# A hybrid attention and convolution layer: the first stage's loads and engine orders laid anew, squares shared between two engines

## The chip, the core and the metric

The kernel runs on one core of a Trainium2 chip. The metric is the device time of one execution in microseconds, here 587.03 as the median of three runs (586.88 to 587.10). A core has five engines with a queue each, and each engine takes its own instructions in order: TensorE (PE; PEld is its weight load), VectorE (DVE), ScalarE (ACT), GpSimd (POOL), and SyncE (SP), which here only issues transfers.

## The reference

One layer over 1024 latent tokens and 256 context tokens, 1024 wide, in fp32. Both inputs are normalised over the row, modulated with a scale and a shift that come from a conditioning vector, and projected; columns go to eight heads of neighbourhood attention and to a gated short convolution.

```python
shift, scale, gate = adaln(c, w_ada, b_ada)
shift_c, scale_c, gate_c = adaln(c_ctx, w_ada, b_ada)
h = rmsnorm(x, norm_g) * (1 + scale[:, None]) + shift[:, None]
hc = rmsnorm(ctx, norm_g) * (1 + scale_c) + shift_c
q, k, v, za, u, bg, cg, zc = jnp.split(h @ w_in, SPLIT_POINTS, axis=-1)
...
attn = neighbourhood_attention(q, k, heads(v), kc, vc, rpb) * jax.nn.silu(za)
conv = gated_short_conv(u, bg, cg, zc, conv_w, conv_b)
x_new = x + gate[:, None] * (jnp.concatenate([attn, conv], axis=-1) @ w_out)
```

Here `rmsnorm` multiplies by the inverse root of the mean of the squares of a row, and `adaln` is a product of a silu with a weight matrix.

## The kernel before

The program has stages: a first one that makes the modulated input `h` and, from it, the first group of convolution columns; projections of the four head pairs (`pacc`, `cacc` for the context); the attention, with the other convolution columns (`pu`) as filler between its steps; the output product (`pout`). The change touches the first stage alone.

**What the first stage computes.** `h` is needed turned, with the 1024 model columns on the partitions, as eight tiles `h0` to `h7` of 128 columns, each with two halves of 512 tokens, and each as a rounded high part and a low remainder, so that three fast products replace one in fp32. The row sums of squares come from the eight token tiles x0 to x7 (`sq`, into `sums0` for the first half and `sums1` for the second; `sums2` is the context's, from n0 and n1). `root` adds a small constant on VectorE and raises to the power -0.5 on POOL; `Rt` spreads the four sums of a half over the partitions by four transposes on TensorE (two for the context), and `R` copies the result out of PSUM on ACT (`rs0`, `rs1`, `rs2`). For each column tile k, `pr` multiplies the conditioning vector with a slab of `w_mod` (64 small matmuls into `tr`), `tp` turns the result on VectorE, and `ab` makes the scale and the shift. Then for half h and tile k: `u` scales the transposed input (the loaded tile `t`, or, for two tiles of the first half, TensorE's own transposes `T` and `v`), `hi` adds the shift and rounds on ACT, `lo` takes the remainder on VectorE.

**The first columns.** Chunk k of the weights (load `c`, rounding `ch` on ACT, remainder `cl` on VectorE) meets `h` in `fc`: `fc` h k i is three matmuls of 512 columns into the banks `acc`, where i is 0 for high by high, 1 for the low weights, and 2 for the low `h`. There are 48 such groups, 144 matmuls. `conv0` evacuates the banks for the convolution: a copy `ub` on ACT and a product `cu` on VectorE for the first half of the tokens, and the same again for the second. Meanwhile the weight chunks of the first `pacc` tile are loaded and split (`q`, `qh`, `ql`), and the rotary tables are loaded (`g`) and multiplied with the gains (`rg`, VectorE).

**What sets the order.** Nothing is scheduled: `LOADS` and `STEPS` (lines 36 to 49) list short words, `do` (line 750) runs them one by one through the table `does` (line 732), and the class `ordered` chains each engine's instructions in that order. A word's loads go into SP's queue where the word stands. Buffers come in rings: three for slabs, six for `xh`, five for weight chunks `wr`, so that a load can also wait for the release of an earlier tile. Words `warm` and `fill` are matmuls on zeros with no use but to keep TensorE busy.

Of the kernel before, what the change touches and what calls it, by code (L numbers as in the profile page):

```python
# [10 lines left out]
F32 = mybir.dt.float32  # L11
F32R = mybir.dt.float32r
BF16 = mybir.dt.bfloat16
AF = mybir.ActivationFunctionType
ALU = mybir.AluOpType
# [4 lines left out]
P = 128  # L20
D = 1024
T = 1024
L = 256
KT = D // P
# [8 lines left out]
TICKS = [2, 3, 3, 4, 4, 4, 4, 1] + [4, 4, 4, 1] + [4, 4, 4, 2] + [4, 4, 4, 1] + 3 * [4, 4, 3, 1] + [3, 2, 3, 1]  # L33
EPS = 1e-6

LOADS = "x0 x1 x2 x3 s0 c0 s1 c1 x4 x5 x6 x7 t10 t11 s2 t02 t12 c2"
STEPS = [
# [11 lines left out]
]  # L49
CONTEXT = "Hi0 Hi1 Lo0 Lo1 Hi2 Hi3 Lo2 Lo3 Hi4 Hi5 Lo4 Lo5 Hi6 Hi7 Lo6 Lo7"  # L50

# [4 lines left out]
def body(tc, es, x, xb, xt, cb_, ct, w_mod, w_gate, b_ada, w_grp, w_col, q_g, k_g, bias, w_out, vecs, cst, out):  # L56
# [21 lines left out]
    pe, act, dve, pool = every = [ordered(e) for e in (nc.tensor, nc.scalar, nc.vector, nc.gpsimd)]  # L78
    sp = ordered(nc.sync)

    def sbuf(name, side=None, bufs=1):
        kw = {} if side is None else {"side": side}
        return tc.tile_pool(name=name, bufs=bufs, reuse_waits="tile", **kw)
# [59 lines left out]
    c2 = cp.tile([P, KT, 2], F32, name="c2")  # L143
    ab = cp.tile([P, KT, 4], F32, name="ab")
    ng, bsh, bsc = vecT[:, 16:24], vecT[:, 24:32], vecT[:, 32:40]
# [12 lines left out]
    def more_h(ks):  # L158
        for k in ks:
            t = place(k, [P, 2, T], F32R, f"h{k}")  # L160
            hh.append(t[:, 0])
            hl.append(t[:, 1])

    cvp = hs.enter_context(sbuf("cvp", side="right"))
# [380 lines left out]
    xp = xs.enter_context(sbuf("xp"))  # L545
# [4 lines left out]
    def tr():  # L550
        return ps0.tile([P, 512], F32, name="tr", tag="tr", bufs=2)

    strict[:] = every + [sp]
    xn, xh, xc, slabs, mods, rows, chunks, pair = {}, {}, {}, {}, {}, {}, {}, []
# [26 lines left out]
    sums = [xp.tile([P, 4], F32, name=f"sums{i}") for i in range(3)]  # L581
    spread_r = [xp.tile([P, 512], F32, name=f"rs{i}") for i in range(2)] + [cxp.tile([P, L], F32, name="rs2")]

    def square(t):

        sqj = xp.tile([P, D], BF16, name="sqj", tag="sqj", bufs=1)
        act.activation(sqj, xn[t], AF.Square, scale=1.0 / 32, accum_out=sums[t // 4][:, t % 4:t % 4 + 1])

    def root(g):

# [4 lines left out]
    def spread_rows(g):  # L595

        n = 4 if g < 2 else 2
        pr = tr()
        for i in range(n):
            pe.transpose(pr[:, i * P:(i + 1) * P], sums[g][:, i:i + 1].broadcast_to([P, P]), ident)  # L600
        return lambda: act.copy(spread_r[g][:, :n * P], pr[:, :n * P])

    def products(k):

        mods[k] = tr()
        for kt in range(KT):
            for g in range(4):
                pe.matmul(mods[k][32 * g:32 * g + 32, :64], c32[:, kt], slabs[k][:, kt, 64 * g:64 * g + 64],
                          start=kt == 0, stop=kt == KT - 1, skip_group_check=True)

    def turned_rows(k):
        rows[k] = xp.tile([P, 64], F32, name="rw", tag="rw", bufs=2)
        dve.transpose(rows[k], mods[k][:, :64])

    def modulation(k):

        a = ab[:, k].rearrange("p (w j) -> p j w", w=2)
        dve.tensor_scalar(a[:, 1], rows[k][:, 32:34], b1[:, k:k + 1], ng[:, k:k + 1], ALU.add, ALU.mult)
        dve.tensor_scalar(a[:, 0], rows[k][:, 0:2], bsh[:, k:k + 1], None, ALU.add)

    scaled = {}

# [39 lines left out]
    def half_of(v, half):  # L662
        return v[:, half * 512:(half + 1) * 512]

    def first_columns(half, k, i):

        wh, wl = chunks[k][:2]
        for u in (0, 2, 1):
            uc = slice(u * P, (u + 1) * P)
            pe.matmul(acc0[u][half], (wl if i == 1 else wh)[:, uc], half_of(hl[k] if i == 2 else hh[k], half),  # L670
                      start=k == 0 and i == 0, stop=k == KT - 1 and i == 2)

    def cast_chunk(raws, k):
        raw = raws[k][:].rearrange("p a b -> p (a b)")
        w = wpp.tile([P, 2, 384], F32R, name="w", tag="w", bufs=12)
        act.copy(w[:, 0], raw)
        raws[k] = raw, w

    def rest_of_chunk(raws, k):
        raw, w = raws[k]  # L680
        dve.tensor_tensor(w[:, 1], raw, w[:, 0].bitcast(F32), ALU.subtract)
        raws[k] = w[:, 0], w[:, 1], w[:, :, P:384]

    ch = {}

# [11 lines left out]
    tables = []  # L697

    def gains(i):

        rw, gqk = tables[0]
        if i == 0:
            pool.tensor_scalar(gqk[:, 0], gqk[:, 0], 0.125, None, ALU.mult)
            pool.tensor_tensor(gkc1[:, 0], gqk[:, 0], gqk[:, 1], ALU.mult)
            tables.append(sl.tile([P, 2, NB, 2, HD], F32, name="rg", tag="slab", bufs=3))
        n, k = divmod(i, 2)
        rraw = rw[:, 512 * n:512 * n + 512].rearrange("p (b d) -> p b d", d=HD)
        dve.tensor_tensor(tables[1][:, n, :, k], rraw, gqk[:, k:k + 1].broadcast_to([P, NB, HD]), ALU.mult)
        if i == 3:
            sp.dma_start(rope_d, tables[1][:].rearrange("p n b k d -> p (n b k d)"))  # L710

    def context_high(k):
# [11 lines left out]
    def keep_clock(n, late=False):  # L724

        v = zeros[:].rearrange("p (o n) -> p o n", o=1).broadcast_to([P, 4, P]) if late else warm
        ps = acc0[1][1][:].rearrange("p (a n) -> p a n", a=4) if late else acc0[1][1]
        for _ in range(n):
            pe.matmul(ps, zeros if late else warm[:, :P], v, start=True, stop=True)
# [4 lines left out]
        "c": lambda k: chunks.update({k: chunk_load(CU, k)}), "q": lambda k: ch.update({k: chunk_load(CQ, k)}),  # L734
        "e": lambda k: load_ct(k), "g": lambda i: tables.append(gains_load()),
        "sq": lambda t: square(t), "root": lambda g: root(g),
        "Rt": lambda g: copies.update({g: spread_rows(g)}), "R": lambda g: copies[g](),
        "pr": lambda k: products(k), "tp": lambda k: turned_rows(k), "ab": lambda k: modulation(k),
        "ch": lambda k: cast_chunk(chunks, k), "cl": lambda k: rest_of_chunk(chunks, k),
        "qh": lambda k: cast_chunk(ch, k), "ql": lambda k: rest_of_chunk(ch, k),  # L740
        "u": lambda h, k: scale((h, k), xh[h, k][:], spread_r[h][:], k, 0) if (h, k) in xh else scale_early(k),
        "T": lambda t: transposed(t), "fill": lambda n: keep_clock(n, True), "v": lambda h, k: normed_early(k), "more": lambda: more_h(range(6, KT)),
        "hi": lambda h, k: shift_high((h, k), half_of(hh[k], h), k, 0),
        "lo": lambda h, k: shift_low((h, k), half_of(hl[k], h), half_of(hh[k], h), k, 0),
        "fc": lambda h, k, i: first_columns(h, k, i), "rg": lambda i: gains(i),
        "warm": keep_clock, "Hi": lambda k: context_high(k), "Lo": lambda k: context_low(k),
        "conv": lambda i: conv_step(),
    }

    def do(steps):  # L750
        for word in steps.split():
            name = word.rstrip("0123456789")
            at = word[len(name):]
            does[name](*([int(at)] if name in ("warm", "fill") else map(int, at)))
# [9 lines left out]
    more_h(range(6))  # L764
    do(LOADS)
    keep_clock(6)
# [357 lines left out]
    tiles, scales, waiting, nxt, raws = {}, {}, [], [], []  # L1124
# [26 lines left out]
    for n in range(NT + 3):  # L1151


        p, t = divmod(n, NB)
# [23 lines left out]
        if t == 0 and 0 < n < NT:  # L1178
            nxt += map(chunk_split, raws)
            ch, nxt, raws = nxt, [], []  # L1180
# [133 lines left out]
    with sbuf("att") as ap, psum("psb") as psb:  # L1314
# [6 lines left out]
        for n in range(len(TICKS)):  # L1321
# [11 lines left out]
            if ready:  # L1333
                p = ready.pop()
# [83 lines left out]
    def four(tags):  # L1418
        return [bank("pout", tag) for tag in tags]
# [65 lines left out]
    a = four("SSCC")  # L1485
    c5 = four("OOUU")
# [29 lines left out]
    c3 = four("OOUU")  # L1516
# [84 lines left out]
```

## Time and profile before

| what | value |
|---|---|
| median of three runs | 587.03 us |
| the profiled execution | 587.34 us |
| its span, first to last instruction | 585.6 us |
| TensorE busy, 0 to 27.23 us | 22.52 us |
| TensorE busy, 27.23 to 63.16 us | 35.69 of 35.93 us |
| TensorE busy, 63.16 us to the end | 519.02 of 522.44 us |
| VectorE and ACT busy, 27.23 to 63.16 us | 28.70 and 18.30 us |
| moved by transfers, 0 to 27.23 us | 364 GB/s |

Durations are those of one execution, read from the hardware profiler. Matmuls are pipelined and their ends are modelled, so that a busy TensorE is not one at its peak, and lengths of single matmuls overlap; start-to-start steps are the better measure. A row of a timeline has the start, the length, engine, line, operation, what it writes and reads, and in brackets the idle time before it with what ended that. In the chain of waits each row is a piece of the chain that ended last: start, length, what. All the helpers' instructions carry one line, so that tiles, not lines, tell them apart.

### The profile page before, as it was taken

To read this page: it belongs to the slowest core of one execution; us is meant where nothing else is said; L and a number is where in the kernel's file an instruction comes from. 1 tells how busy PE (TensorE), PEld (TensorE's weight loads), DVE (VectorE), ACT (ScalarE), POOL (GpSimd) and SP (SyncE) were. 2 spreads that over 40 slices of the span, in tenths; PEclk is the share of its full clock that TensorE was granted. 3 is DMA by queue.
4 is the path that set the end of the run, shared out by engine and by line. 5 is a ranking of instruction groups with operands and counts; after the bars stand their busy time and mean duration, and the time that the engine had idled before them with its cause. 6 is when DMAs were issued, how large, how long until landed. Compare 5 with 4: busy or idle time off the path is not lost.

```text
span 585.6 us, 9903 instructions
## 1 busy us (share of the span) xinstructions
PE 577.2 (99%) x3531; PEld 483.3 (83%) x3532; DVE 438.6 (75%) x890; ACT 282.0 (48%) x653; POOL 57.4 (10%) x82
## 2 busy tenths in 40 slices
PE   8899999999999999999999999999999999999997
PEld 4578999999999999988878787878787867888886
DVE  1578879656846746367998788998979887999952
ACT  5636355336525545433463474466535646643420
POOL 1001033123223232100000000000000001100000
PEclk9999999999999999999999999999999999999999
DMA  8997666845756695686253646564758273773532
GB/s 323 410 415 278 220 229 211 283 166 194 267 189 213 224 341 205 226 297 219 73 209 120 243 140 229 182 216 155 254 187 257 80 263 96 248 252 89 199 125 91
DMA packets 66679, 126.14 MB, mean 215 GB/s; under 512 B 8714, under 2 KB 27650, under 8 KB 64325
## 3 DMA queue, kind: packets, MB, share of 16 engines
q1 hardware_dynamic: 66244, 124.70, 60.8%
q0 software_dynamic: 384, 0.81, 0.6%
q8 instruction: 28, 0.46, 0.3%
q14 instruction: 23, 0.18, 0.1%
HBM read 92.38 MB, written 33.10 MB: 214 GB/s over the span
## 4 chain that ended last, share of the span: by engine, by line
PE 91%; DMA 5%; DVE 2%; ACT 1%; SPq 0%; issue 0%; POOL 0%; DVEq 0%; ACTq 0%
PE pu L71 29%; PE pacc L71 23%; PE pout L71 13%; PE acc L71 5%; PE po L71 5%; PE cacc L71 4%; PE pss L71 3%; DMA xn<-in_xb 3%; PE pc L71 3%; PE pmx L71 2%; PE trA L71 1%; PE tr L71 1%; DMA y_d<-tb 1%; PE ptot L71 1%; PE trB L71 1%; DVE sb L71 0%
## 5 line engine op out<-in xcount | busy, mean ns | idle before, releaser
L71 PE MATMUL pu<-h,uh 128*128 128x512 f32 x544 | 174.4, 402 | 0.0
L71 PE MATMUL pacc<-w,h 128*128 128x384 f32 x768 | 138.5, 337 | 0.0
L71 PEld LDWEIGHTS pacc<-w,h 128*128 128x128 f32 x768 | 132.8, 188 | 0.2
L71 PEld LDWEIGHTS pu<-h,uh 128*128 128x128 f32 x544 | 97.3, 188 | 18.4 <-issue 1.2
L71 PE MATMUL pu<-h,ul 128*128 128x512 f32 x272 | 106.5, 391 | 0.0
L71 PE MATMUL pout<-right,left 128*128 128x512 f32 (+2 forms) x348 | 77.0, 383 | 0.0
L71 PEld LDWEIGHTS pout<-right,left 128*128 128x128 f32 x348 | 64.4, 188 | 12.7
L71 PEld LDWEIGHTS pu<-h,ul 128*128 128x128 f32 x272 | 51.1, 188 | 11.5
L71 POOL TENSOR_TENSOR ss<-ss,few 128x4 f32<-128x4 f32 (+1 forms) x40 | 41.4, 1035 | 127.0 <-DVE ss L71 126.7
L71 ACT COPY sc<-pc 128x512 f32<-128x512 f32 x32 | 18.7, 587 | 44.6 <-PE pc L71 44.6
L71 PE MATMUL acc<-h,w 128*128 128x512 f32 x144 | 35.3, 397 | 1.4 <-ACT h L71 1.4
L71 ACT ACTIVATE sc<-sc 128x512 f32<-128x512 f32 x32 | 20.3, 633 | 33.7 <-DVE sc L71 33.6
L71 ACT ACTIVATE sq<-pacc 128x256 f32<-128x256 f32 x32 | 12.3, 386 | 47.4 <-PE pacc L71 46.7
L71 DVE TENSOR_TENSOR sum<-sum,sb 128x372 f32<-128x372 f32 (+2 forms) x64 | 31.1, 485 | 2.7
L71 PEld LDWEIGHTS acc<-h,w 128*128 128x128 f32 x144 | 26.3, 188 | 7.8 <-ACT h L71 2.1
L71 DVE SCALAR_TENSOR_TENSOR m<-pout,ab,m 128x512 f32<-128x512 f32 (+2 forms) x34 | 22.9, 717 | 13.0 <-PE pout L71 12.9
L71 ACT ACTIVATE qn<-pacc,ss 128x64 f32<-128x64 f32 x128 | 30.0, 330 | 4.8 <-PE trA L71 2.5
L71 DVE TENSOR_TENSOR mx<-mx,sb 128x372 f32<-128x372 f32 (+2 forms) x64 | 30.8, 481 | 1.4
L71 DVE TENSOR_REDUCE ss<-sq 128x4 f32<-128x260 f32 (+1 forms) x40 | 15.7, 393 | 21.5 <-ACT sq L71 21.5
L71 DVE TENSOR_TENSOR ul<-uraw,uh 128x512 fp32r<-128x512 f32 x34 | 23.1, 685 | 10.0 <-ACT uh L71 10.0
L71 DVE TENSOR_TENSOR sb<-pss,bt 128x192 f32<-128x192 f32 (+3 forms) x48 | 27.5, 600 | 2.3 <-PE pss L71 2.2
L71 DVE TENSOR_TENSOR qs<-trA,qs 128x512 fp32r<-128x512 f32 x16 | 11.1, 691 | 21.2 <-ACT qs L71 20.2
(142 smaller groups left out, 862.8 us busy)
## 6 DMA issues: line engine op xcount, KB each, us to landing
uraw<-in_w_col SPq DMA_DIRECT2D x34, 256.0 KB, 3.8
slab<-in_w_mod SPq DMA_DIRECT2D x8, 1024.0 KB, 9.0
q_d<-qs SPq DMA_DIRECT2D x32, 256.0 KB, 4.0
k_s<-k_d SPq DMA_DIRECT2D x8, 1024.0 KB, 6.9
q_s<-q_d SPq DMA_DIRECT2D x16, 512.0 KB, 3.9
wr<-in_w_grp SPq DMA_DIRECT2D x40, 192.0 KB, 5.0
bt<-in_rpb SPq DMA_DIRECT2D x8, 564.0 KB, 6.8
xn<-in_xb SPq DMA_DIRECT2D x8, 512.0 KB
```

The lines of the kernel that those rows point to most:

```text
L71: i = emit(*a, **kw)
```

## The change

The first stage's two lists are written anew. Every word of the old lists stands in the new ones, but for the words `warm` and the number of `fill`; new is a word `sh`, the addition of the shift, which was part of `ab`. Three places show the kind of the change in the code:

```diff
-LOADS = "x0 x1 x2 x3 s0 c0 s1 c1 x4 x5 x6 x7 t10 t11 s2 t02 t12 c2"
+LOADS = "x0 x1 x2 x3 s0 c0 s1 x5 c1 x6 x4 x7 t10 c2 s2 t02"
 STEPS = [
...
-    "conv0 R2 rg1 rg2 rg3 ql7",
...
+    "qh4 ql6 fc171 ql4 conv0 qh3 fc170 ql3 qh7 qh5 ql7 fc172 ql5 conv0 root2 Rt2 rg3 R2",
 ]
...
-        sqj = xp.tile([P, D], BF16, name="sqj", tag="sqj", bufs=1)
-        act.activation(sqj, xn[t], AF.Square, scale=1.0 / 32, accum_out=sums[t // 4][:, t % 4:t % 4 + 1])
+        total = sums[t // 4][:, t % 4:t % 4 + 1]
+        if t in (1, 3, 5, 7):
+            sqv = cvp.tile([P, T + 2], F32, name="sqv", tag="cu", bufs=1)
+            dve.scalar_tensor_tensor(sqv[:, :D], xn[t], 1.0 / D, xn[t], ALU.mult, ALU.mult, accum_out=total)
+        else:
+            sqj = xp.tile([P, D], BF16, name="sqj", tag="sqj", bufs=1)
+            act.activation(sqj, xn[t], AF.Square, scale=1.0 / 32, accum_out=total)
...
         dve.tensor_scalar(a[:, 1], rows[k][:, 32:34], b1[:, k:k + 1], ng[:, k:k + 1], ALU.add, ALU.mult)
-        dve.tensor_scalar(a[:, 0], rows[k][:, 0:2], bsh[:, k:k + 1], None, ALU.add)
+
+    def shift(k):
+        a = ab[:, k].rearrange("p (w j) -> p j w", w=2)
+        act.activation(a[:, 0], rows[k][:, 0:2], AF.Identity, bias=bsh[:, k:k + 1])
...
+    done = [0, 0]
+
     def first_columns(half, k, i):
...
-                      start=k == 0 and i == 0, stop=k == KT - 1 and i == 2)
+                      start=done[half] == 0, stop=done[half] == 3 * KT - 1)
+        done[half] += 1
```

The last piece lets the groups `fc` of a half stand in any order: the first one that comes starts the sum in its banks. The gains' function likewise does its preparations at the first `rg` that comes and its store behind the fourth.

What the lists make of the engines' orders is shown at three places. In the rows, `acc00` and `acc01` are the banks of the first and the second half of the tokens for one column group (`acc10`, `acc11`, `acc20`, `acc21` for the others), and numbers behind an underscore count buffers.

TensorE, around the transposes of the second half's sums (`sums1`), before and then with the change:

```order
L71 MATMUL tr_425<-ci_106,sums1_162 128x128 x4
L71 MATMUL tr_435<-slab_202,c32_223 32x64 x32
L71 MATMUL acc01_157<-h0_170,w_321 128x512
L71 MATMUL acc21_158<-h0_170,w_321 128x512
L71 MATMUL acc11_160<-h0_170,w_321 128x512
```
```order
L70 MATMUL tr_420<-ci_106,sums1_162 128x128 x4
L70 MATMUL acc00_155<-h1_171,w_382 128x512
L70 MATMUL acc20_156<-h1_171,w_382 128x512
L70 MATMUL acc10_159<-h1_171,w_382 128x512
L70 MATMUL tr_435<-slab_202,c32_219 32x64 x32
L70 LDWEIGHTS zeros_116
L70 MATMUL acc11_160<-zeros_116 128x512
L70 MATMUL acc01_157<-h0_170,w_250 128x512
```

A group of three matmuls of the first half, the last of tile `h1`, has moved from ahead of these transposes to behind them; the product with the third slab stays ahead of the second half's first matmul.

TensorE, from the transposes of the context's sums (`sums2`) on, before (they stand among the groups of `h6`, with one more group of `h6` and the six of `h7` behind them), and then with the change, where the end of the last group of `h7` and the first `pacc` tile are shown:

```order
L71 MATMUL acc11_160<-h6_262,w_776 128x512
L71 MATMUL tr_898<-ci_106,sums2_163 128x128 x2
L71 MATMUL acc01_157<-h6_262,w_776 128x512
L71 MATMUL acc21_158<-h6_262,w_776 128x512
L71 MATMUL acc11_160<-h6_262,w_776 128x512
L71 MATMUL acc00_155<-h7_263,w_854 128x512
```
```order
L70 MATMUL acc01_157<-h7_255,w_704 128x512
L70 MATMUL acc21_158<-h7_255,w_704 128x512
L70 MATMUL acc11_160<-h7_255,w_704 128x512
L70 MATMUL tr_956<-ci_106,sums2_163 128x128 x2
L70 MATMUL pacc_1003<-w_691,h0_170 128x384 x3
L70 MATMUL pacc_1003<-w_829,h1_171 128x384 x3
```

The two transposes have moved from the middle of the last groups to the seam between the first stage and the second.

VectorE, where the context's sum stands (`TENSOR_SCALAR sums2`), before and then with the change:

```order
L71 SCALAR_TENSOR_TENSOR hw_799<-xh_569,ab_119,rs0_164 128x512
L71 TENSOR_SCALAR sums2_163<-sums2_163 128x2
L71 SCALAR_TENSOR_TENSOR hw_806<-xh_576,ab_119,rs1_165 128x512
L71 SCALAR_TENSOR_TENSOR h6_262<-hw_799,ab_119,h6_262 128x512
L71 SCALAR_TENSOR_TENSOR h6_262<-hw_806,ab_119,h6_262 128x512
```
```order
L70 TENSOR_TENSOR rg_900<-rw8_791 128x8x64 x2
L70 TENSOR_TENSOR w_896<-wr_787,w_896 128x384
L70 TENSOR_TENSOR w_923<-wr_837,w_923 128x384
L70 TENSOR_TENSOR cu_930<-acc20_156,ub_933 128x2x16x16
L70 TENSOR_TENSOR w_936<-wr_819,w_936 128x384
L70 TENSOR_TENSOR w_942<-wr_834,w_942 128x384
L70 TENSOR_TENSOR w_944<-wr_789,w_944 128x384
L70 TENSOR_TENSOR cu_930<-acc21_158,ub_951 128x2x16x16
L70 TENSOR_SCALAR sums2_163<-sums2_163 128x2
L70 TENSOR_TENSOR rg_900<-rw8_791 128x8x64
```

The sum has moved from between the two scalings of `h6` to behind the second product `cu`, which reads the finished bank of the second half.

On SP, the loads of the last weight chunks and of the tables stand behind the load of q1, whose buffer the remainder of chunk 5 (`cl5`) frees; `cl5` now stands behind `tp6` on VectorE, and the order of the words there is `tp6 sh6 cl5 q1 t07 n1 n0 t17 q6 q5 g0`.

More of the change, by code (lines that the diff above doesn't have):

```diff
@@ L663, in half_of @@
         return v[:, half * 512:(half + 1) * 512]
+    done = [0, 0]
     def first_columns(half, k, i):
-        wh, wl = chunks[k][:2]
+        raw, w = chunks[k]
+        wh, wl = w[:, 0], w[:, 1]
         for u in (0, 2, 1):
@@ L681, in rest_of_chunk @@
         dve.tensor_tensor(w[:, 1], raw, w[:, 0].bitcast(F32), ALU.subtract)
-        raws[k] = w[:, 0], w[:, 1], w[:, :, P:384]
+        if raws is ch:
+            ch[k] = w[:, 0], w[:, 1], w[:, :, P:384]
     ch = {}
@@ L701, in gains @@
         rw, gqk = tables[0]
-        if i == 0:
+        if len(tables) == 1:
             pool.tensor_scalar(gqk[:, 0], gqk[:, 0], 0.125, None, ALU.mult)
@@ L708, in gains @@
         dve.tensor_tensor(tables[1][:, n, :, k], rraw, gqk[:, k:k + 1].broadcast_to([P, NB, HD]), ALU.mult)
-        if i == 3:
+        tables.append(i)
+        if len(tables) == 6:
             sp.dma_start(rope_d, tables[1][:].rearrange("p n b k d -> p (n b k d)"))
@@ L737, in body @@
         "Rt": lambda g: copies.update({g: spread_rows(g)}), "R": lambda g: copies[g](),
-        "pr": lambda k: products(k), "tp": lambda k: turned_rows(k), "ab": lambda k: modulation(k),
+        "pr": lambda k: products(k), "tp": lambda k: turned_rows(k), "ab": lambda k: modulation(k), "sh": lambda k: shift(k),
         "ch": lambda k: cast_chunk(chunks, k), "cl": lambda k: rest_of_chunk(chunks, k),
```

19 rows, old and new, of the table STEPS are left out of this document.

## The prediction

> **What bounds the kernel now.** I read the page first, then TensorE's waits, the chain of waits over the first 66 us, and last VectorE's timeline around the end of that stretch. The page says that TensorE is busy throughout:
>
> ```profile
> span 585.6 us, 9903 instructions
> ...
> PE 577.2 (99%) x3531; PEld 483.3 (83%) x3532; DVE 438.6 (75%) x890; ACT 282.0 (48%) x653; POOL 57.4 (10%) x82
> ```
>
> Asked for everything that TensorE waited for from 63 us to the end, the trace has one row:
>
> ```profile
> PE pmx L71 <- DVE rm L71: 0.4, 1, 0.4
> ```
>
> So behind 63 us there is 0.4 us of waiting in 522. The changed code ends near 63 us, and whatever it moves the start of the second stage (the tile `pacc`) by should arrive at the end undiminished, in either direction. The question is when `pacc` starts. The chain of waits has today's answer (start, length, what):
>
> ```profile
> 9.45 12.32 DMA xn<-in_xb
> ...
> 21.85 1.16 ACT sqj L71 x2
> ...
> 23.04 0.18 DVE sums L71
> ...
> 23.29 1.03 POOL sums L71
> ...
> 24.36 0.66 PE tr L71 x4
> ...
> 25.05 0.59 ACT rs L71
> ...
> 25.66 0.76 DVE hw L71
> ...
> 26.45 0.73 ACT h L71
> ...
> 27.23 3.01 PE acc L71 x12
> ...
> 31.25 0.24 issue
> ...
> 52.83 1.03 PE tr L71 x64
> 53.86 4.30 PE acc L71 x18
> 58.16 0.22 PE tr L71 x2
> 58.38 4.78 PE acc L71 x21
> 63.16 2.97 PE pacc L71 x17
> ```
>
> Up to 27.23 the last token tile of the first half of the loads sets the pace: it lands at 9.45 + 12.32 = 21.77, then its square (ACT), the sum (DVE), the power (POOL), four transposes (PE), a copy, a scaling and a rounding follow one another. From 27.23 to 63.16 TensorE runs without a gap but the 0.24. The transfer is late because the queue is full: 399 to 416 GB/s (last column) from 5 us on.
>
> ```profile
> 0.00:5.00 5.00, 3.48 (x10) 1.20 (x11) 0.38 (x2) 2.92 (x4) 1.24 (x10) 1.00 0.50 162
> 5.00:10.00 5.00, 5.00 (x29) 2.69 (x28) 0.01 (x1) 4.11 (x9) 0.00 (x0) 1.00 1.03 399
> 10.00:15.00 5.00, 4.37 (x84) 2.37 (x84) 1.75 (x4) 1.66 (x4) 1.03 (x1) 1.00 1.02 416
> 15.00:20.00 5.00, 4.07 (x76) 3.10 (x77) 4.26 (x12) 3.79 (x6) 0.00 (x0) 1.00 1.02 411
> ```
>
> **The front.** The new order of loads puts x4 to x7 and c1 in another order among themselves, but the same transfers stand ahead of x7, which stays the fourteenth. It lands at 21.77 again. Its square is now VectorE's. No row shows a two-source VectorE operation of 1024 elements. The nearest are these:
>
> ```profile
> 70.47 0.87 DVE L71 SCALAR_TENSOR_TENSOR hw<-xc,ab,rs 128x256 f32<-128x256 f32 x2
> ```
> ```profile
> 57.41 1.41 DVE L71 SCALAR_TENSOR_TENSOR h<-hw,ab,h 128x512 fp32r<-128x512 f32 x2
> 58.74 1.02 DVE L71 TENSOR_TENSOR w<-wr,w 128x384 fp32r<-128x384 f32 x2
> 61.32 0.69 DVE L71 TENSOR_TENSOR cu<-acc,ub 128x512 f32<-128x512 f32 x1 [1.56 <-ACT ub L71]
> 61.93 1.49 DVE L71 TENSOR_TENSOR w<-wr,w 128x384 fp32r<-128x384 f32 x3
> 63.43 0.69 DVE L71 TENSOR_TENSOR cu<-acc,ub 128x512 f32<-128x512 f32 x1
> 64.04 1.88 DVE L71 TENSOR_TENSOR rg<-rw 128x512 f32<-128x512 f32 x3
> 65.84 0.55 DVE L71 TENSOR_TENSOR w<-wr,w 128x384 fp32r<-128x384 f32 x1
> ```
>
> A 256-element one is about 0.44, a 512-element one 0.70, so 1024 elements are bounded by 2 x 0.65 = 1.3 and 4 x 0.44 = 1.76; I take 1.4, against 1.16 on ACT: **+0.25**. What then runs up to the first matmul of the second half is the same chain, and as much useful work stands ahead of that matmul as before (18 `acc` matmuls, three products with a slab); one group of three only moves from ahead of the four transposes to behind them. So that matmul starts at 27.5. The work behind it is the same too: 63.16 - 27.23 = 35.93, less the 0.24 gap (I find no wait at this place, the loads being as early as before) and less the 0.22 for the two transposes, which now stand behind: the last `acc` matmul ends at 27.5 + 35.47 = **62.95**, 0.2 before today's.
>
> The shift additions that go to ACT cost nothing, ACT being busy 48%; they save VectorE 0.13 each (the step from 49.08 to 49.21 here), all of it beside TensorE's work:
>
> ```profile
> 48.60 0.25 DVE L71 STREAM_TRANSPOSE rw<-tr 128x64 f32<-128x64 f32 x1 [0.61 <-PE tr L71]
> 48.88 0.29 DVE L71 TENSOR_SCALAR ab<-rw,b,vecT 128x2 f32<-128x2 f32 x1
> 49.08 0.22 DVE L71 TENSOR_SCALAR ab<-rw,vecT 128x2 f32<-128x2 f32 x1
> 49.21 0.75 DVE L71 SCALAR_TENSOR_TENSOR hw<-xh,ab,rs 128x512 f32<-128x512 f32 x1
> ```
>
> **The end of the stage is what costs.** The two transposes of the context sums (`Rt2`) stood seven matmul groups ahead of `pacc`, fed by a sum that VectorE made at about 50 us. Now they stand between the last `acc` matmul and `pacc`, and the sum stands in VectorE's queue behind the second `cu` product. TensorE runs in order, so `pacc` waits for the sum, for POOL's power and for the transposes. When does VectorE get there? Its tail starts with the transpose of the last slab's rows (`tp7`), which needs the last product with a slab. Behind that product stand ten groups of three matmuls, 30 x 4.30/18 = 7.17, so it ends at 62.95 - 7.17 = 55.8. From there, by start-to-start steps of the rows above: transpose 0.28, gain 0.20, two scalings 2 x 0.67, `lo07` (its rounding on ACT, 0.73, lies beside the second scaling) 0.67 plus about 0.2 of waiting, which is 58.5. Then a `rg` 0.60, `lo17` 0.67, two `rg` 1.20, two `w` 1.00, `cu` 0.61, three `w` 1.50, `cu` 0.61: 6.19, so the sum starts at 64.7. From a sum to POOL is 23.29 - 23.04 = 0.25, from POOL to the transposes 24.36 - 23.29 = 1.07, and the transposes take 0.22: `pacc` at **66.25**, 3.1 after today's 63.16.
>
> One more thing can hold this tail. The first `rg` now waits for the table load, which stands on SP behind q1, whose buffer is freed only by VectorE's split of chunk 5, now behind `tp6`. By the same count back from the last slab product (its own 1.03, nine groups 6.45) `tp6` is at 48.3 and the split ends at 49.1. Behind it go seven loads, 2.16 MB or 5.3 us at 410 GB/s, two small ones, and the table, 1.3 us: not before 55.7. Issue to use took this long today:
>
> ```profile
> 45.89 0.42 SPq L71 DMA_DIRECT2D rw<-in_cst  x1
> ```
> ```profile
> 52.46 0.48 POOL L71 TENSOR_SCALAR rw<-rw 128x64 f32<-128x64 f32 x1 [1.22 <-DMA rw<-in_cst]
> ```
>
> That is 6.6 us; issued at about 52.8 the table lands at 59.4 at the latest. With POOL's 0.48 and 0.25 more, `rg` can start between 56.5 and 60.1, and VectorE gets there at 58.5: between nothing and 1.6 lost. The late end is the row nearest to it, but its queue was fuller; I take **+0.3**.
>
> Sum: 3.1 + 0.3 = +3.4. The profiled execution lasted 587.34 (span 585.6), 0.31 over the median of 587.03; added to each, 590.7 and 590.4. I predict the median, **590.4**.
>
> **The rivals.**
> The shortest wait: VectorE is ahead of my count and only what cannot be avoided is left. The `ub` copy follows the last write of its bank, two matmuls (0.48) before the end, 0.62 later `cu` (60.70 to 61.32 today), 0.61 the sum, 0.25, 1.07, 0.22: 62.95 + 2.29 = 65.24, +2.1, **589.1**. Against it: VectorE's queue as counted.
>
> ```profile
> 60.70 0.59 ACT L71 COPY ub<-acc 128x512 f32<-128x512 f32 x1 [0.23 <-PE acc L71]
> ```
>
> The table is late by the full 1.6: **591.7**.
>
> The array slows after the gap. Its first matmuls took 2.74/6 = 0.457 each, those after 4.48 only 3.20/14 = 0.229:
>
> ```profile
> 1.52 2.74 PE L71 MATMUL acc<-warm 128*128 128x512 bf16 x6 [1.52 <-POOL warm L71]
> ...
> 4.48 3.20 PE L71 MATMUL acc<-warm 128*128 128x512 bf16 x14
> ```
>
> An idle stretch from 62.95 to 66 could bring that state back; the loss would be what the start lost, 2.74 - 6 x 0.229 = 1.4: **591.8**. No gap over 0.7 us follows the start today, so the trace doesn't show how long one must be; all columns of granted clock read 1.00. [...]
>
> The other side: the second square sum was held by ACT and not by the landing that the trace puts at 21.77. ACT's square before it began here,
>
> ```profile
> 20.59 1.06 ACT L71 ACTIVATE sqj<-xn 128x1024 bf16<-128x1024 f32 x1
> ```
>
> and with 1.16 for one with its read of the sum it ended at 21.75. With two engines the front would gain up to the landing itself. The fourteen transfers are 6.78 MB; the four windows above moved 6.94 by 20.0, so x7 cannot be in before 19.6: at most 2.2 earlier, all stages shifted alike, **588.2**, and 586.9 with the shortest wait. It decides once the first matmul of the second half starts before 25.0. Against it: the chain names the transfer there, although by 0.02 us only.
>
> That the wait is not built is excluded: the rows of the order put the transposes directly ahead of `pacc`.
>
> **How the numbers follow.** The forecast 0.58, the shortest wait 0.12, late table 0.08, slow array 0.11, the front 0.11. The range reaches from below the shortest wait, 588.7, to above the slow array, 592.3; outside lie the front and a little of two costs together. A measurement of this kernel can tell about 0.2% from no change, 1.2 us, so "same" ends at 588.2. Of the front's 0.11, 0.08 are within it and 0.03 below, where both gains come together; 0.01 is added for what I don't see. Faster 0.04, same 0.08, slower 0.88.
>
> **What would show it.** In the new profile: first matmul of the second half at about 27.5; last `acc` matmul near 63 with no gap after 27.5; the two transposes at about 66 with the idle time ahead of them put down to POOL `sums`, some 3 us; the sum on VectorE directly behind the second `cu`, and no idle time on VectorE from `tp7` to it but for the table; behind 67 us no new TensorE wait. I am wrong if `pacc` starts before 65, or if TensorE waits at other places between 27 and 63.

## The result and the profile after

| what | before | with the change |
|---|---|---|
| median (runs) | 587.07 us (4: 586.88 to 588.14) | 594.20 us (4: 593.09 to 594.53) |
| ratio | 1 | 1.0114 [1.0096, 1.0132] |
| profiled execution, span | 587.34, 585.6 us | 593.09, 591.2 us |
| mean granted clock of the runs | 0.999 in the profiled one | 0.997, 0.994, 0.991, 0.991 |
| `pacc` starts at | 63.16 us | 67.25 us |
| its first 72 matmuls take | 12.50 us | 14.00 us |

The kernel is slower by 1.1%, as forecast in sign, but by twice the amount: 7.1 us where 3.4 were predicted, and outside the range that was given. The page of the changed kernel already differs in one slice of its clock row:

```profile
span 591.2 us, 9893 instructions
...
PE 578.8 (98%) x3528; PEld 484.1 (82%) x3528; DVE 443.3 (75%) x890; ACT 279.4 (47%) x653; POOL 56.2 (9%) x82
...
PEclk9999899999999999999999999999999999999999
```

A slice is 14.8 us; the fifth, from 59 to 74 us, has an 8. TensorE's busy time went up by 1.6 us with no more useful work to do: the same work took longer, which the lower clock explains, and idle time has to be looked for apart from it. It is in TensorE's waits from 27 us to the end (total, times, longest):

```profile
PE tr L70 <- POOL sums L70: 3.9, 1, 3.9
PE pmx L70 <- DVE rm L70: 0.4, 1, 0.4
PE acc L70 <- ACT h L70: 0.2, 1, 0.2
```

There is one new wait, of 3.9 us, at the transposes that now stand at the seam. Nothing else is new behind 27 us; the 0.4 at `pmx` was there before. The end of the chain of waits (start, length, what) gives the two parts of the loss:

```profile
64.83 0.60 DVE cu L70
65.44 0.09 DVE sums L70
...
65.66 1.04 POOL sums L70
...
66.74 0.51 PE tr L70 x2
67.25 14.00 PE pacc L70 x72
81.25 5.55 PE cacc L70 x32
```

Before, the same two last rows read:

```profile
63.16 12.50 PE pacc L71 x72
75.66 5.55 PE cacc L71 x32
```

`pacc` starts 67.25 - 63.16 = 4.09 later, and its first 72 matmuls take 1.50 more; `cacc` then starts 81.25 - 75.66 = 5.59 later, and the span is 5.6 longer. So the whole loss of the profiled execution is made between 63 and 81 us, and arrives at the end undiminished. The windows of 1 us say what the 1.50 are (the columns: stretch, its length, busy time of PE, PEld, DVE, ACT, POOL, granted clock, DMA share, GB/s):

```profile
65.00:66.00 1.00, 0.00 (x0) 0.00 (x0) 1.00 (x3) 0.00 (x0) 0.34 (x1) 1.00 0.00 0
66.00:67.00 1.00, 0.26 (x3) 0.26 (x3) 0.10 (x1) 0.00 (x0) 0.69 (x1) 0.98 0.13 57
67.00:68.00 1.00, 1.00 (x5) 1.00 (x4) 0.00 (x0) 0.71 (x2) 0.10 (x1) 0.50 1.06 451
68.00:69.00 1.00, 1.00 (x5) 1.00 (x5) 0.52 (x1) 1.00 (x2) 0.00 (x0) 0.50 0.97 401
69.00:70.00 1.00, 1.00 (x5) 1.00 (x4) 0.96 (x3) 0.12 (x1) 0.00 (x0) 0.50 0.36 139
70.00:71.00 1.00, 1.00 (x6) 1.00 (x5) 0.90 (x3) 0.00 (x0) 0.00 (x0) 0.81 0.06 16
71.00:72.00 1.00, 1.00 (x7) 1.00 (x7) 1.00 (x2) 0.00 (x0) 0.34 (x1) 1.00 0.40 49
```

Right behind the gap the clock is 0.50. From the means of the mixed slices it fell at 66.96 (0.98 is 0.04 us at half) and rose at 70.38 (0.81 is 0.38 us at half): 3.4 us, and nearly half of the work of that time is lost. TensorE is busy throughout these windows, with five matmuls touching each of them where seven or eight do at the whole clock; no list of waits shows that.

### The profile page after: what moved, and what is told of

It reads as the page before. It is cut to its first block, busy times and chain, and to the rows that moved or that the text cites. A ratio compares the mean times of both kernels' runs of the same rounds, so it can differ in the third digit from the quotient of the medians.

```text
span 591.2 us, 9893 instructions
## 1 busy us (share of the span) xinstructions
PE 578.8 (98%) x3528; PEld 484.1 (82%) x3528; DVE 443.3 (75%) x890; ACT 279.4 (47%) x653; POOL 56.2 (9%) x82
## 4 chain that ended last, share of the span: by engine, by line
PE 87%; DMA 6%; DVE 3%; ACT 1%; SPq 1%; issue 1%; POOL 0%; DVEq 0%; ACTq 0%; POOLq 0%
PE pu L70 29%; PE pacc L70 23%; PE pout L70 13%; PE po L70 5%; PE cacc L70 4%; PE pss L70 3%; DMA xn<-in_xb 3%; PE pc L70 3%; PE pmx L70 2%; PE acc L70 2%; PE trA L70 1%; DMA xh<-in_xt 1%; DMA wr<-in_w_grp 1%; DMA y_d<-tb 1%; PE tr L70 1%; PE ptot L70 1%
## 5 line engine op out<-in xcount | busy, mean ns | idle before, releaser
L70 PE MATMUL pacc<-w,h 128*128 128x384 f32 x768 | 140.1, 340 | 0.0
L70 PEld LDWEIGHTS pacc<-w,h 128*128 128x128 f32 x768 | 134.3, 190 | 0.1
L70 DVE TENSOR_TENSOR sb<-pss,bt 128x192 f32<-128x192 f32 (+3 forms) x48 | 27.5, 602 | 2.3 <-PE pss L70 2.2
```

The lines of the kernel that those rows point to most:

```text
L70: i = emit(*a, **kw)
```

## The experiments

Three readings of the 4.09 + 1.50 are weighed: **S**, all of it comes from the place of the context's sum and its two transposes at the seam (a wait, then the halved clock); **F**, part of it comes from the front (the squares on VectorE, the order of the first loads); **L**, part of it comes from the late table and the rest of the lists.

**The sum moved ahead, the transposes before the last group.** On the changed kernel, two words:

```diff
-    "... sq8 rg1 fc071 fc072 rg0 fc070",
-    "qh4 ... ql3 qh7 qh5 ql7 fc172 ql5 conv0 root2 Rt2 rg3 R2",
+    "... sq8 rg1 root2 fc071 fc072 rg0 fc070",
+    "qh4 ... ql3 qh7 Rt2 qh5 ql7 fc172 ql5 conv0 rg3 R2",
```

> The changed kernel, with the context's sum moved up in VectorE's queue (ahead of the last groups of the first stage) and its two transposes moved ahead of the last group, so that nothing at the seam waits for them. Theory S (the whole loss is the wait at the seam, about 4 us, and the halved clock after it, 1.5 us for each window): 587.0 within 0.6, clock 0.999, no TensorE wait between 62 and 68 us. Theory L (the late loads of the last weight chunks and tables hold the tail): pacc still waits for VectorE's splits, 588 to 590. Theory F (the front: squares on two engines, idle stretches there and clock drops they cause): 590 or more, clock below 0.998.

Measured: 588.54 us (10 runs, 587.11 to 588.99), 1.0019 [1.0009, 1.0028]. The ten runs have mean clocks of 0.997 to 1.000. Most of the loss is gone, but about 1.1 us of it stay. In this kernel's trace, VectorE's, POOL's and TensorE's timelines have (start, length, engine, what, and in brackets the idle time before it):

```profile
60.92 0.68 DVE L70 TENSOR_TENSOR rg<-rw 128x512 f32<-128x512 f32 x1
61.52 1.01 DVE L70 TENSOR_TENSOR w<-wr,w 128x384 fp32r<-128x384 f32 x2
```
```profile
61.08 2.03 POOL L70 TENSOR_TENSOR sums<-sums,few 128x2 f32<-128x2 f32 x1 [3.02 <-DVE sums L70]
```
```profile
63.17 0.43 PE L70 MATMUL tr<-ci,sums 128*128 128x128 f32 x2 [1.06 <-POOL cu L70]
```

POOL's power lasts 2.03 us, where the same instruction took 1.03 to 1.04 at the seam of the changed kernel, and the transposes wait 1.06 for it. It runs beside the rest of an `rg`, two `w` and a `cu` of VectorE; at the seam only the rest of an `rg` ran beside it. The expectation had reckoned with 1.0, and that is its miss: the power ends 1 us later than was reckoned, and the transposes stood too early by that much.

**The same early sum, the transposes left at the seam.** Against the changed kernel only `root2` has moved:

```diff
-    "... sq8 rg1 fc071 fc072 rg0 fc070",
-    "... ql5 conv0 root2 Rt2 rg3 R2",
+    "... sq8 rg1 root2 fc071 fc072 rg0 fc070",
+    "... ql5 conv0 Rt2 rg3 R2",
```

> The changed kernel, with the context's sum early in VectorE's queue and its transposes at the seam as in the changed kernel, so that POOL, which took 2.0 us for the power beside VectorE's work, is done when they come up. S: pacc directly behind the last acc group at about 63.3 us, 587.3 within 0.6: the rest of the change is worth nothing either way. If the rest of the change costs or saves something: 588.5 or more, 586.4 or less.

Measured: 587.31 us (11 runs, 586.76 to 588.19), 0.9999 [0.9990, 1.0007]. The chain of waits of this kernel:

```profile
60.95 0.17 DVE sums L70
...
61.19 2.04 POOL sums L70
...
63.29 0.42 PE tr L70 x2
63.71 12.50 PE pacc L70 x72
```

The power takes 2.04 again, but now it ends at about the end of the last group. With everything else of the change in place, one word's place in VectorE's queue makes up the 7 us, and the rest of the change, the new front included, is worth nothing that can be measured in either direction. That is against F and L.

**The squares alone**, on the kernel before: the two branches of the diff's `square`, nothing else.

```diff
+        if t in (1, 3, 5, 7):
+            dve.scalar_tensor_tensor(sqv[:, :D], xn[t], 1.0 / D, xn[t], ALU.mult, ALU.mult, accum_out=total)
+        else:
             act.activation(sqj, xn[t], AF.Square, scale=1.0 / 32, accum_out=total)
```

> The kernel before, with the squares of every second token tile on VectorE and nothing else. If the landing of x7 sets the front, as the chain says: 587.3, within 0.3 of before (VectorE's square with its read of the sum took 1.24 us against ACT's 1.16). If ACT's run of squares held it: 585 to 586.5.

Measured: 587.59 us (11 runs, 587.02 to 588.27), 1.0003 [0.9995, 1.0012]; `pacc` starts at 63.45, 0.29 later than before in the profiled execution. The squares are not where the time went, and nothing was gained by them either; that too is against F. What holds the front is not shown by this experiment: here VectorE comes to the last square at 21.97 straight from other work, and the chain of waits runs through TensorE's own queue (19 `acc` matmuls, ten of them on zeros, from 20.53 to 25.15). In the changed kernel it can be seen: VectorE stands idle for 1.36 us until the last token tile has landed at 21.76, and in eight profiles with the changed lists, where it landed between 21.28 and 22.18, the first matmul of the second half came 5.85 to 5.86 later each time.

**The kernel before, with the seam of the change.** The other direction: the two words and nothing else of the change.

```diff
-    "sq9 tp6 ... fc150 root2 u16 ..."
-    "... u17 hi07 Rt2 ql1 q6 fc162 hi17 lo07",
-    "conv0 R2 rg1 rg2 rg3 ql7",
+    "sq9 tp6 ... fc150 u16 ..."
+    "... u17 hi07 ql1 q6 fc162 hi17 lo07",
+    "conv0 root2 Rt2 R2 rg1 rg2 rg3 ql7",
```

> The kernel before, with that one move alone: the context's sum behind the second cu product, its transposes behind the last acc group. S: pacc starts 2.3 to 2.6 us later, 589.5 if the clock holds, 591 to 592.5 if the gap of 2.4 us halves it for one window or two. F or L: 587.2, no difference worth the name.

Measured: 590.28 us (4 runs: 589.92, 589.11, 590.64, 591.07, with mean clocks of 0.999, 1.000, 0.996, 0.997), 1.0049 [1.0034, 1.0064]. Its chain:

```profile
62.97 0.59 ACT ub L71
...
63.59 0.69 DVE cu L71
64.28 0.08 DVE sums L71
...
64.50 1.04 POOL sums L71
...
65.59 0.43 PE tr L71 x2
66.02 12.52 PE pacc L71 x72
```

Here VectorE has little else queued, and the wait is the least that this place allows: copy, `cu`, sum, power, transposes follow one another, and `pacc` is 2.86 late, a little more than the 2.3 to 2.6 expected. In the profiled execution the clock stayed whole (72 matmuls in 12.52); the two runs with a mean clock of 0.996 and 0.997 are the slowest. The two words alone thus make the kernel slower by about 3 us. One row of VectorE in this profile bears on the first experiment:

```profile
64.26 1.89 DVE L71 TENSOR_TENSOR rg<-rw 128x512 f32<-128x512 f32 x3
```

POOL's power ran from 64.50 to 65.54 beside these three products and took 1.04 all the same. So the power was not longer beside every product of VectorE. Beside `w` alone it was: in the front of the changed kernel, on 128x4, it took 1.25 us beside two `w` and 1.03 where VectorE was idle. Beside `cu` alone no run shows it.

**The seam filled.** The changed kernel, with sixteen matmuls on zeros, into a bank that is free, ahead of the two transposes. The wait for the sum stays, TensorE is not idle in it.

```diff
-    "... ql5 conv0 root2 Rt2 rg3 R2",
+    "... ql5 conv0 root2 seam16 Rt2 rg3 R2",
...
+    def keep_seam(n):
+        v = zeros[:].rearrange("p (o n) -> p o n", o=1).broadcast_to([P, 4, P])
+        ps = tr()[:].rearrange("p (a n) -> p a n", a=4)
+        for _ in range(n):
+            pe.matmul(ps, zeros, v, start=True, stop=True)
...
```

> The changed kernel, with 16 matmuls on zeros between the last acc group and the two transposes, into a free bank; the wait itself stays. S: pacc starts at about 67 us as in the changed kernel, but the granted clock stays 1.00 behind it and its first 72 matmuls take 12.5 us instead of 14.0; 591.3 within 0.6 and clock 0.999 in all runs. If the clock loss doesn't come from the gap (F): 594 and clock 0.991 to 0.997.

Measured: 590.87 us (4 runs: 590.36, 591.32, 591.78, 590.41), 1.0066 [1.0049, 1.0083]; mean clocks 1.000, 1.000, 0.997, 0.999. The chain of the first of them:

```profile
64.69 0.09 DVE sums L70
...
64.92 1.04 POOL sums L70
...
66.00 0.43 PE tr L70 x2
66.43 12.50 PE pacc L70 x72
```

The 72 matmuls take 12.50 again: in this execution the slow stretch is gone when TensorE is kept busy in the gap, though nothing useful is done in it. Of the four runs one still has a mean clock of 0.997, which was not expected. What stays, `pacc` at 66.43, is the wait by itself.

**The gap halved.** The changed kernel with `root2` directly behind the first `conv0`, so that the sum waits for one `cu` and not for two:

```diff
-    "... ql4 conv0 qh3 fc170 ql3 qh7 qh5 ql7 fc172 ql5 conv0 root2 Rt2 rg3 R2",
+    "... ql4 conv0 root2 qh3 fc170 ql3 qh7 qh5 ql7 fc172 ql5 conv0 Rt2 rg3 R2",
```

> The changed kernel, with the context's sum directly behind the first cu product, so that the gap at the seam is about 2 us instead of 3.9. S: pacc at about 65.2 us; 590.6 if a gap of 2 us still halves the clock for one window, 589.1 if it doesn't. F or L: 592 or more.

Measured: 590.93 us (4 runs: 589.89, 590.52, 591.96, 591.34; mean clocks 1.000, 0.999, 0.993, 0.996), 1.0062 [1.0046, 1.0078]. From the chain of the first of these executions:

```profile
63.39 1.84 POOL sums L70
...
65.27 0.43 PE tr L70 x2
65.70 12.51 PE pacc L70 x72
```

The gap is 2.5 us and the power takes 1.84 beside VectorE's products. With the whole clock the time is that of a wait of 2.5; the two runs with the lower clocks are 0.8 to 2.1 us above the two others. So a gap of 2.5 us seems to be followed by a low clock in some executions and not in others; this rests on the mean clock and the time alone, as no execution with the low clock was caught in a profile here.

**The changed kernel again**, in six, one and one more runs, to see how its executions differ.

> The changed kernel once more, for its spread over executions. If the seam is all there is, every execution has the gap of about 4 us, and the times differ by whole half-rate windows of 3.4 us (1.5 us of pacc each): 592.5 to 594.6, clock 0.991 to 0.997. If the clock is also lost elsewhere, the granted clock over the first 30 us is below 1.00 in the profile.

Measured: 592.49 us (6 runs), 1.0083 [1.0067, 1.0099]. Five of them have clocks of 0.993 to 0.997 and took 592.35 to 593.71; the sixth has a clock of 1.000 and took 590.29, like the kernel with the filled seam. The profiled one shows the picture of the first: `pacc` at 66.97, its first 72 matmuls in 13.99.

> The changed kernel unchanged, one look, in search of an execution with a mean clock under 0.996. One window at half rate of 3.41 us lowers the mean clock of a 591 us span by 0.0029, so 0.994 is two windows and 0.991 three. If the further windows belong to the seam, the profile shows the first 72 pacc matmuls longer than 14.0 (up to 15.5). If they belong to the front, where the tensor engine waits 1.7 us in pieces for the first two sums and 1.2 us for the token tiles, a granted clock of 0.5 shows between 9 and 30 us and the first matmul of the second half starts later than 27.7. Time 592.3 to 594.5; with 0.997 or more nothing is told apart.

> As the third look at the changed kernel: the same kernel, the same two readings, the same numbers.

Measured: 593.70 us at a mean clock of 0.997, and 594.12 at 0.994. The first has `pacc` at 67.74 and its first 72 matmuls in 14.07, one slow stretch. The chain of the second, and its windows of 1 us:

```profile
66.02 1.04 POOL sums L70
...
67.10 0.69 PE tr L70 x2
67.79 14.83 PE pacc L70 x72
```
```profile
63.00:64.00 1.00, 0.18 (x1) 0.00 (x0) 1.00 (x3) 0.89 (x2) 0.00 (x0) 1.00 0.03 12
...
65.00:66.00 1.00, 0.00 (x0) 0.00 (x0) 1.00 (x4) 0.00 (x0) 0.00 (x0) 0.95 0.00 0
66.00:67.00 1.00, 0.00 (x0) 0.00 (x0) 0.46 (x1) 0.00 (x0) 0.98 (x1) 0.50 0.00 0
...
72.00:73.00 1.00, 1.00 (x5) 1.00 (x5) 1.00 (x3) 0.00 (x0) 0.81 (x1) 0.64 0.82 156
```

The clock fell at 65.90, inside the gap (63.18 to 67.10), and rose at 72.72: 6.82 us, two times 3.41. The second stretch at a clock of 0.50 lies directly behind the first, at the seam, and not at the front. The first of the two still held 1.2 us of the gap; the 72 matmuls lose 2.33 us. In the three other profiles of the changed kernel, with one slow stretch, the fall came 0.22 to 0.55 us after the gap's end. So which of the two kinds an execution is goes with where the fall comes.

**The front filled, the seam open.** Thirteen more matmuls on zeros at the places where TensorE waits in the front:

```diff
-    "T1 sq2 sq1 T2 sq0 T0 T3 ch0 ..."
-    "fc012 fill12 Rt1 ..."
+    "T1 sq2 sq1 fill4 T2 sq0 T0 fill4 T3 ch0 ..."
+    "fc012 fill17 Rt1 ..."
```

> The changed kernel with the same fillers on zeros at the front as in the run with both places filled (4, 4 and 5 matmuls more), and an open seam. If the further windows belong to the front, all clocks are 0.996 or more and the time is 592.3 to 593.1, within 0.5 of one another. If they belong to the seam, clocks of 0.994 and 0.991 stay, with times up to 594.5. The fillers may also stall an engine queue as they did in the run with both filled (0.66 us at 31 us), then each number is up to 0.9 higher.

Measured: 594.46 us (4 runs, 594.00 to 596.27; mean clocks 0.997, 0.994, 0.996, 0.993), 1.0128 [1.0105, 1.0152]. The low clocks stay, so they are not the front's. The profile shows one slow stretch, at the seam again:

```profile
67.00:68.00 1.00, 0.00 (x0) 0.00 (x0) 0.50 (x1) 0.00 (x0) 0.95 (x1) 0.81 0.00 0
...
68.83 13.55 PE pacc L70 x72
```

The clock fell at 67.62, 0.52 us before the gap's end at 68.14, and was whole again from 71.02 on: with 0.52 us of the gap in it the first stretch was the only one, with 1.2 us a second followed. The time is a little longer than without the fillers, and the chain of waits shows why:

```profile
29.88 0.91 PE tr L70 x55
30.79 1.26 issue
32.05 0.35 PE tr L70 x9
```

In the middle of the third product with a slab TensorE stands for 1.26 us with nothing that the profile shows to wait for. Before it was 0.24 at this place; one of the profiles of the changed kernel has 0.37 a little further on, among the `acc` matmuls, and the others have none.

**Both filled.** The fillers of the last experiment and the sixteen at the seam:

> The kernel with the filled seam, and with more matmuls on zeros in the idle stretches of the front too (13 more ahead of and between the transposes of the token tiles and ahead of the second sum's). If single half-rate windows that the filled seam still showed (0.997 in one of four) come from the front: clock 0.999 or 1.0 in all runs, 590.5 with a spread under 0.6. If not: as with the filled seam alone, 590.4 to 591.8.

Measured: 591.87 us (4 runs, 591.63 to 592.21), 1.0075 [1.0062, 1.0088]. The clocks are 0.999 to 1.000 in all four, and the spread is small, as expected; the time is 1.4 above what was expected. The sum on VectorE stands at 66.04 in place of 64.69 in the kernel with the seam alone filled, and `pacc` starts at 67.78 in place of 66.43. Of these 1.35 us 0.47 are the landing of the last token tile, which came at 21.75 and not at 21.28 in this execution; the rest arises at the third slab product, with the same stop at "issue", here 0.66 us at 30.85. What makes that stop longer when fillers are added ahead of it was not tried.

No version was found that beats both kernels: the early sum with the transposes at the seam ties with the kernel before.

## Why the prediction went wrong in its size

**What held.** The bound, the place and the mechanism. The first matmul of the second half was put at 27.5 and came at 27.62; the last `acc` matmul was put at 62.95 and ended at 62.89; between them there is no wait of more than 0.2 us; the one new wait is at the seam, on POOL's `sums`, and the sum stands behind the second `cu`; behind the seam no wait is new. The square on VectorE was put at 1.4, from 0.44 and 0.70 for shorter forms, and took 1.24 (first row below: 1.22, and 0.08 for the read of the sum). VectorE's tail was counted row by row, and can be compared so:

```profile
21.86 1.22 DVE L70 SCALAR_TENSOR_TENSOR sqv<-xn 128x1024 f32<-128x1024 f32 x1 [1.36 <-DMA xn<-in_xb]
...
55.86 0.25 DVE L70 STREAM_TRANSPOSE rw<-tr 128x64 f32<-128x64 f32 x1 [1.22 <-PE tr L70]
...
58.38 0.75 DVE L70 SCALAR_TENSOR_TENSOR h<-hw,ab,h 128x512 fp32r<-128x512 f32 x1 [0.48 <-ACT h L70]
59.33 0.69 DVE L70 TENSOR_TENSOR rg<-rw 128x512 f32<-128x512 f32 x1 [0.20 <-DMA rw<-in_cst]
...
65.35 0.16 DVE L70 TENSOR_SCALAR sums<-sums 128x2 f32<-128x2 f32 x1
```

| step | predicted | measured |
|---|---|---|
| `tp7` starts | 55.8 | 55.86 |
| VectorE reaches the first `rg` | 58.5 | 59.13 |
| it waits there for the table | 0.3 | 0.20 |
| from that `rg` to the sum | 6.19 | 6.02 |
| sum to power, power to transposes | 0.25, 1.07 | 0.31, 1.08 |
| transposes until `pacc` | 0.22 | 0.51 |
| `pacc` starts | 66.55 | 67.25 |

**What was off by a little: the wait.** It was 4.09 in place of 3.4. Of the difference 0.63 came before the first `rg`: the wait of `lo07` for its rounding on ACT was 0.48 and not 0.2, and smaller steps went the same way. 0.29 came from the transposes, which were costed as two in a running queue: at the seam, or ahead of the last group, they take 0.42 to 0.43 even at the whole clock, in the kernels with the early sum and with the filled seam; here, where the clock fell within them, 0.51. The other steps gave some 0.2 back. In the other three profiles of the changed kernel `pacc` starts at 66.97, 67.74 and 67.79; a single execution does not fix this term to better than 0.4, and a good part of that is the landing of the last token tile (21.48, 21.41 and 22.18 there, 21.76 here). With the wait right and nothing else, the forecast would have been 591.1.

**The step that failed: the sum has no term for the clock.** The prediction saw that the array could slow after the gap, and priced one stretch closely: "the loss would be what the start lost, 2.74 - 6 x 0.229 = 1.4", against 1.50 in the first profile. That the two agree so well is in part luck: the slow start lasted 2.74 us, the stretch at the seam 3.4. But it made a rival of it, with a chance of 0.11. That chance was the author's estimate and no row or run shows it; of the profile before the prediction itself says: "No gap over 0.7 us follows the start today, so the trace doesn't show how long one must be". The runs showed in its place a low clock nearly every time: of the twelve executions of the changed kernel eleven have a mean clock of 0.991 to 0.997; one has 1.000. The term belonged into the sum, at 1.5 for one slow stretch and 2.33 for two; five of the twelve have mean clocks of 0.991 to 0.994, as two slow stretches or more would give (an estimate: 3.41 us at a clock of 0.50 lower the mean of a span of 591 us by 0.0029). With the wait's own 0.7 these make the miss: 590.4 + 0.7 + 1.5 = 592.6 for one slow stretch, 593.4 for two, give or take the 0.4 of the wait; the eleven lie at 592.35 to 594.53, and the one at a clock of 1.000 at 590.29.

Two things were not in the forecast. The gap was longer (3.86 to 4.20 us idle in the four profiles, some 3 us forecast), and the time before the fall was not idle throughout. In the execution with two slow stretches the clock fell at 65.90, and in the 3.41 us before it, as long as one slow stretch, the last `acc` matmuls ran until 63.18: 0.69 us of work did not keep the clock up. In the one with `pacc` at 67.74 it fell at 67.86, 0.55 us after TensorE had started again. How long a gap must be for the clock to fall, and how much work would keep it up, was not measured. By the experiments a gap of 2.2 or 2.5 us may already do it: there clocks of 0.993 to 0.997 came in two of four runs each, but these executions were not seen in a profile, so that this is inferred from the mean clock alone, which is weak evidence (see below).

**The rivals.** The shortest wait (+2.1) did not come: VectorE had work to the end. It came in the kernel before with the two words moved, as +2.86. The late table cost 0.2 and not 1.6. The front gave nothing: the squares alone are 1.0003 [0.9995, 1.0012], the whole new front with the early sum 0.9999 [0.9990, 1.0007], and in the changed kernel the last token tile landed at 21.76, as before, with VectorE idle ahead of it. That the landing holds the front, as the chain's 0.02 us had said, is what these rows show for the changed kernel.

**What stays open.** Three slow stretches, as a mean clock of 0.991 would be by that estimate (two runs, 594.1 and 594.5), were not seen in a profile; nor was the run at 0.997 of the kernel with the filled seam, whose seam has 0.08 us of idle time on TensorE in the profiled run. In the first experiment, whose wait is 1.06 us, two runs at 0.997 (588.76 and 588.98) took no longer than two at 0.999 and 1.000 (588.74 and 588.99). A mean clock of 0.997 thus seems possible without a loss of time; some of the clock goes at the very end, where the profile of the kernel before has 0.97 from 580 to 585 us. This weakens what the clocks of the 2.2 and 2.5 us gaps are taken for. The cause of the stop named "issue" in the third slab product is open too.

## What to carry to other kernels

A chain of small steps through three engines (sum, power, transposes) cost its whole length here, with `pacc` 4.09 us later, when its last link was put at a seam where the bounding engine has nothing else to do; started some groups earlier in the queue of the engine that begins it, it cost nothing (0.9999 [0.9990, 1.0007]). The gap in TensorE's work, 3.9 to 4.2 us, had a second price behind it that no list of waits shows, 1.50 us on 72 matmuls in the first profile: look at the granted clock and at the length of a known group of matmuls behind a gap, and put that price into the sum, not among the rivals, when the gap is near the length of the one here, where eleven of twelve executions had the low clock. When a gap can't be removed, matmuls on zeros in it can take away the second price and leave the first, as they did here in the profiled run (the 72 matmuls in 12.50 us again, `pacc` still at 66.43).

## What the runs showed of the hardware

- In the five profiles that have it, a gap of 3.9 to 4.2 us on TensorE was followed by 3.40 to 3.42 us or 6.82 us at a clock of 0.50, counted from the fall. Where the fall came 1.2 us before the gap's end, a second stretch followed the first; where it came 0.52 us before it, none did. 72 matmuls took 13.55 to 14.07 and 14.83 us in place of 12.50.
- In the 3.41 us before such a fall, as long as one slow stretch, TensorE had worked for up to 0.69 us.
- POOL's power on a tile of 128x2 took 1.03 to 1.04 us at the seam of the changed kernel, where only the rest of one `rg` (0.4 us) ran beside it, and 1.84 to 2.04 us where VectorE ran `w` and `cu` at the same time (on 128x4 in the front of the changed kernel 1.25 beside two `w`, and 1.03 where VectorE was idle). Beside three `rg` in a row it took 1.04. VectorE's products did not become longer by it: two `w` took 1.01 beside it and 1.02 before. The expectation of the first experiment left the delay out.
